# Query sums of squares fed into the projection stream, and rotary steps on 1024 columns

## The chip, the core and the metric

The kernel runs on one core of a Trainium2 chip. The metric is the device time of one execution in microseconds (us); the median of three runs is shown. PE is the matrix engine and PEld its weight loads, DVE the vector engine, ACT the scalar engine, POOL and SP the two other engines, which here issue transfers (DMAs) almost alone. Each engine works through its own queue in order, and a wait at the head of a queue holds up all that stands behind it.

## The reference, cut to what matters

One decoder layer on 1024 tokens of width 1024. The input is RMS-normalised and multiplied by one wide matrix (projections). Two mixers read the result:

```
# A: dilated attention, three groups (window, dilation) of 8 heads of 64
q_a, k_a = rope(q), rope(k)      # t * cos + rotate_half(t) * sin, per token position
o_a = sum over groups of softmax(q_a k_a^T / 8) v, weighted by the softmax denominators
# B: gated delta rule, 8 heads of 64, chunks of 64 tokens
gq = silu(conv(q)) / norm(gq) / 8 ; gk = silu(conv(k)) / norm(gk) ; gv = silu(conv(v))
t_inv = inverse(1 + a)           # a: unit lower triangular part of a chunk, 64 x 64
o_b = sequential scan over 16 chunks ; then RMS norm
merged = sigmoid(gate_a) * up_a(o_a * silu(z_a)) + sigmoid(gate_b) * up_b(o_b * silu(z_b))
out = rmsnorm(x + merged @ w_out)
```

The norm of gq needs a sum of squares over 64 channels for each head and token. In the rotary step, a head's 64 channels are two halves a and b: the results are a cos - b sin and b cos + a sin.

## The kernel before, in words

Matrices are split into two float16 parts, high and low, and each product is three matmuls. The projections are cut into *units* of 256 output columns. A unit is a generator; one *tick* of the `Feed` runs its next step: three matmuls on 512 columns in a unit of 28 steps (`Seven`, which forms seven products in place of eight) or in one of 32 (`Normal`). A unit's weights come by DMA on POOL's queue, and DVE and ACT split them (`whi`, `wlo`).

PE's order is written out by hand: what the code emits first runs first. Between steps of attention, of the delta rule's preparation and of its scan, the code calls `feed.tick(n)`, so the projections fill the time in which PE would wait for DVE and ACT. `feed.later(n, fn)` hangs a piece of work into the stream n ticks later, and `feed.flush()` ticks until nothing hangs there. The other engines' queues are ordered by a scheduler that goes by order in the code and by `high_priority`.

**Rotary step** (`rope_evict`, `rope_half`, L583 to L608). A unit of queries or keys gives four PSUM tiles of 512 columns: two halves of tokens, and in each the channel halves a and b. Each tile is copied out by ACT (`SC.copy`), or in a `Seven` unit with a remainder by DVE, into a buffer `rx` (three of 512 columns). For each half of the tokens DVE then does four products with the tables, two sums, and, for the results A and B each, ACT casts to float16 with the tokens reordered for the group's dilation (4 or 8: the source is read with a stride), and DVE subtracts the cast from the source, read with the same stride. There are 12 units and so 24 halves. `rope_out` sends the pieces by 16 and more DMAs on SP's queue.

**Attention** (`att_run`) runs the six sets of heads as a pipeline of scores, softmax (L776, L780), transposes (L790, L795) and values. In the last two sets `combine` merges the three groups on DVE, and `turn_out` (L876) transposes the result on PE `TURN_LAG` ticks after the set's values.

**Delta rule.** After attention and its flush, `decay`, `keys_side` and `solve` prepare the chunks; `solve` is a chain of small DVE steps at low priority, once per half of the heads, with a round trip through DRAM: `u_d` and `t_d` are stored and read back as `MT` (L1284) and `T1p` (L1282). `merge` (L1299, L1314) multiplies these on PE. The order of the code around the queries of half hb is:

```
state_side(0)                                  # loads, merge(0), products
for hb in 0, 1:
    feed.until(("gdn", hb, 0)); feed.tick(Q_LAG[hb])
    pairs(hb, qT, E[hb]); spill(hb)            # two times: 64 matmuls L1215, 4 ticks
    sumsq(hb, qT, rq...)                       # four times: 4 transposes L1196, square, sum, 2 ticks
    if hb == 0: feed.tick(STATE_LAG); state_side(1)
```

`sumsq` transposes into the PSUM tag "S" (two banks), ACT squares in place (L1201), DVE sums (L1202). The factors it gives are used in the scan, after its first tile of 128 tokens.

Of the kernel before, what the change touches and what calls it, by code (L numbers as in the profile page):

```python
# [10 lines left out]
F32 = mybir.dt.float32  # L11
# [3 lines left out]
ALU = mybir.AluOpType  # L15
# [42 lines left out]
ZS = 1  # L58
SCAN_LEAD = 6
OG = 2  # L60
TURN_LAG = 16
SUMS_AT = (4, 36, 68, 100)
MERGE_TICKS = 5
V_GAP = 8
# [12 lines left out]
def hybrid_block(ctx: ExitStack, tc: tile.TileContext, A):  # L77
# [498 lines left out]
    tabs = rp.tile([128, 2, S], F32, name="tabs")  # L576
    nc.sync.dma_start(out=tabs, in_=A["tabs"])
    amask = ap.tile([128, 384], F32, name="amask")
    nc.sync.dma_start(out=amask, in_=A["amask"])
    DIL = (1, 4, 8)  # L580

    def rope_evict(p, ct, offset=None, rest=None):
        with tc.high_priority(offset=offset):  # L583
            x = rp.tile([128, 512], F32, name="rx", tag="rx", bufs=3)
            if rest is None:
                SC.copy(x, p)  # L586
            else:
                STT(x, p, -1.0, rest, ALU.mult, ALU.subtract)
        return x

    def rope_half(g, pt, hf, ab, offset=0):
        d = DIL[g]
        ts = slice(hf * 512, hf * 512 + 512)
        with tc.high_priority(offset=offset):
            cos, sin = tabs[:, 0, ts], tabs[:, 1, ts]
            for n, (u, v, op) in (("A", (0, 1, ALU.subtract)), ("B", (1, 0, ALU.add))):
                t1 = rp.tile([128, 512], F32, name="rt1", tag="rt1", bufs=1)
                t2 = rp.tile([128, 512], F32, name="rt2", tag="rt2", bufs=1)
                TT(t1, ab[u], cos, ALU.mult)
                TT(t2, ab[v], sin, ALU.mult)  # L600
                o = rp.tile([128, 512], F32, name="ro", tag="ro", bufs=2)
                TT(o, t1, t2, op)
                ov = o.rearrange("p (n r) -> p r n", r=d)
                nn = 512 // d
                dst = [pt[n + x].rearrange("p (r n) -> p r n", r=d)[:, :, hf * nn:hf * nn + nn]
                       for x in "hl"]
                SC.copy(dst[0], ov)
                TT(dst[1], ov, dst[0], ALU.subtract)  # L608

    def rope_out(pt, pieces):  # L610

        with tc.high_priority():
            for name, dst, r0, _ in pieces:
                for hd in range(4):
                    nc.sync.dma_start(out=dst[r0:r0 + 32, hd], in_=pt[name][32 * hd:32 * hd + 32])
            for _, dst, r0, twice in pieces:
                if twice and r0:
                    nc.sync.dma_start(out=dst[64:128], in_=dst[0:64])

    def rope_tiles():  # L620
        return {n: rp.tile([128, S], F16, name=f"pc{n}", tag=f"pc{n}", bufs=1) for n in ("Ah", "Al", "Bh", "Bl")}

    def rope_unit(g, tiles, what):
        def start():
            pt = rope_tiles()
            pieces = pieces_of(tiles(), what)
            ab = {}

            def out(c, hf, p, rest=None):
                ab[c, hf] = rope_evict(p, c, rest=rest)  # L630
                if (1 - c, hf) in ab:
                    rope_half(g, pt, hf, [ab[0, hf], ab[1, hf]])
                if len(ab) == 4:
# [12 lines left out]

        return gen, gen7

    def rope_first(g, ws, pieces):

        pts = [rope_tiles(), {}]
        for n in "AB":
            both = ap.tile([128, 2, S], F16, name=f"pk{n}", tag="Vh" if n == "A" else "Vl", bufs=2)
            pts[1][n + "h"], pts[1][n + "l"] = both[:, 0], both[:, 1]
        for pt, banks in zip(pts, qk):
            rope_half(g, pt, 0, [rope_evict(p, ct, 0) for ct, p in enumerate(banks)], 0)
        ab = [q, [bank("S", 2), bank("S", 2)]]
        for i, u in ((2, 1), (3, 0), (3, 1)):
            for ct in range(2):
                quarter(ab[u][ct], ws[u], ct, i)  # L660
            if u == 0:

                with tc.high_priority():
                    for n in range(2):
                        feed.units[0][1].split(n)
        for pt, banks in zip(pts, ab):
            rope_half(g, pt, 1, [rope_evict(p, ct) for ct, p in enumerate(banks)])
        for pt, pc in zip(pts, pieces):
            rope_out(pt, pc)

# [16 lines left out]
    def v_unit(g, tiles):  # L687
        def start():
            vs = [ap.tile([128, 8, 256], F16, name=n, tag=n, bufs=2) for n in ("Vh", "Vl")]
            tiles().extend(vs)  # L690
            return vs

        def gen(w):
            wh, wl = w
            Vh, Vl = start()
            for jj in range(4):
                p = bank("mm", 3)
                for u in range(2):
# [12 lines left out]

        def gen7(w):
            vs = start()

            def out(c, hf, p, rest):
                cs = slice(128 * c, 128 * c + 128)
                vh, vl = [v[:, 4 * hf:4 * hf + 4, cs] if g == 0 else
                          v.rearrange("p (r h) c -> p r h c", h=2)[:, :, hf, cs] for v in vs]
                p = p.rearrange("p (i c) -> p i c", c=128)
                with tc.high_priority():  # L720
                    if rest is not None:
                        rest = rest.rearrange("p (i c) -> p i c", c=128)
                        x = rp.tile([128, 4, 128], F32, name="vx", tag="ro", bufs=2)
# [207 lines left out]
    def sums_of_h(k):  # L931

        x = {}
        for i in range(2):
            for j in range(2):
                x[i, j] = rp.tile([128, 512], F32, name="hx", tag=f"rt{j + 1}" if i == 0 else "ro", bufs=1 if i == 0 else 2)
# [252 lines left out]
    def sumsq(hb, src, dst, take=None):  # L1189

        for t0 in range(0, 8, 2):
# [11 lines left out]
            feed.tick(2)  # L1203

    def pairs(hb, src, dst):

# [396 lines left out]
    fp = ctx.enter_context(tc.tile_pool(name="fin", bufs=1))  # L1603
    late.append(fp)
# [243 lines left out]
def _constants():  # L1848
# [14 lines left out]
    ang = (np.arange(S, dtype=f)[:, None] * inv[None, :]).astype(f).astype(np.float64)  # L1863
    sc = H_SCALE * P_SCALE
    tabs = np.stack([np.tile(np.cos(ang).T, (4, 1)), np.tile(np.sin(ang).T, (4, 1))], axis=1) * sc
    q = p[:, None]
    k = p[None, :]
    prev = np.where(k >= q, 0.0, NEG)
# [81 lines left out]
```

## Time and profile before

| | |
|---|---|
| runs | 1096.77, 1093.91, 1096.39 us; median 1096.39 |
| profiled execution | 1097.13 us, of which the span of the trace is 1095.4 |
| PE busy | 1055.7 us, 96% |
| DVE busy | 871.8 us, 80% |
| ACT busy | 572.1 us, 52% |
| granted TensorE clock, mean | 0.995 |

The trace's times run from the start of the span. A row of a group of instructions gives count, busy time, mean duration in ns and the idle time just before them with what ended it. Matmuls overlap in PE, so a busy PE can hold short gaps, and the rows of waits give only those that left it idle.

### The profile page before, as it was taken

What the parts mean: (1) busy time and instruction counts of PE and PEld (TensorE: products, weight loads), DVE (VectorE), ACT (ScalarE), POOL (GpSimd) and SP (SyncE); (2) the same over time, 40 slices, a digit from 0 to 9 for tenths busy, and PEclk for the clock granted to TensorE, in tenths of its full rate; (3) what the DMA queues carried; (4) which work ended last, traced back from release to release, by engine and by line L of the source; (5) the groups of instructions that cost most, each with busy time, mean ns of one, the idle gap of its engine ahead of it and who ended that gap; (6) DMA issues with size and microseconds to landing.
All of it is one profiled execution on the core that took longest, in us unless ns stands there. A gap on an engine that the chain in (4) does not pass through costs nothing.

```text
span 1095.4 us, 23858 instructions
## 1 busy us (share of the span) xinstructions
PE 1055.7 (96%) x9426; PEld 641.1 (59%) x9426; DVE 871.8 (80%) x2039; ACT 572.1 (52%) x1296; POOL 65.4 (6%) x115
## 2 busy tenths in 40 slices
PE   6999999999999999989999999998999999999997
PEld 5895585775866855765555554544545554444443
DVE  5798997969879789979975797966478779699944
ACT  6455766667666656547745624234344335343522
POOL 1200000000000000000000000110200000000000
PEclk9999999999999999999999999999999999999999
DMA  8134521622626332641233357766585532763131
GB/s 290 62 94 138 137 64 66 165 81 81 146 67 164 82 115 75 153 111 56 74 121 138 97 137 186 238 214 174 156 280 159 159 113 88 256 224 127 69 131 77
DMA packets 99344, 146.89 MB, mean 134 GB/s; under 512 B 31120, under 2 KB 64400, under 8 KB 98336
## 3 DMA queue, kind: packets, MB, share of 16 engines
q1 hardware_dynamic: 68976, 83.10, 26.4%
q0 software_dynamic: 12320, 44.11, 13.1%
q10 hardware_dynamic: 17936, 18.16, 4.9%
q8 instruction: 74, 1.21, 0.5%
q14 instruction: 38, 0.31, 0.1%
HBM read 89.56 MB, written 36.90 MB: 115 GB/s over the span
## 4 chain that ended last, share of the span: by engine, by line
PE 57%; DVE 29%; ACT 7%; DMA 3%; issue 3%; SPq 1%; ACTq 0%; DVEq 0%
PE ps_mm L181 14%; PE ps_mm L183 13%; PE ps_mm L182 13%; DVE rt L85 3%; DVE wlo L82 3%; DVE ca L82 2%; DVE sm L776 2%; DVE tl L85 2%; DVE ro L85 2%; ACT sm L780 2%; DVE pcAl L85 1%; PE ps_S L183 1%; PE ps_S L182 1%; PE ps_S L181 1%; DVE pcBl L85 1%
## 5 line engine op out<-in xcount | busy, mean ns | idle before, releaser
L183 PE MATMUL ps_mm<-h_hi,wlo 128*128 128x512 f16 (+1 forms) x552 | 208.0, 377 | 0.0
L182 PE MATMUL ps_mm<-h_lo,whi 128*128 128x512 f16 (+1 forms) x492 | 185.3, 377 | 0.8 <-DVE h_lo L85 0.8
L181 PE MATMUL ps_mm<-h_hi,whi 128*128 128x512 f16 (+1 forms) x492 | 185.6, 377 | 0.0
L183 PEld LDWEIGHTS <-wlo 128*128 128x128 f16 x788 | 77.1, 98 | 87.7 <-issue 1.6
L182 PEld LDWEIGHTS <-whi 128*128 128x128 f16 x848 | 83.1, 98 | 71.6 <-issue 4.7
L181 PEld LDWEIGHTS <-whi 128*128 128x128 f16 x848 | 83.2, 98 | 70.6 <-issue 0.3
L181 PE MATMUL ps_mm<-whi,h_hi 128*128 128x256 f16 x384 | 105.7, 275 | 0.0
L182 PE MATMUL ps_mm<-wlo,h_hi 128*128 128x256 f16 x384 | 105.3, 274 | 0.0
L183 PE MATMUL ps_mm<-whi,h_lo 128*128 128x256 f16 x384 | 105.3, 274 | 0.0
L780 ACT ACTIVATE sm<-sm,osb 128x128 f32<-128x128 f32 (+1 forms) x160 | 69.7, 437 | 54.4 <-DVE osb L776 47.7
L85 DVE TENSOR_TENSOR tl<-ps_G,th 128x256 f16<-128x256 f32 (+1 forms) x96 | 51.9, 541 | 19.1 <-ACT th L795 19.0
L85 DVE TENSOR_TENSOR rt<-rx,tabs 128x512 f32<-128x512 f32 x96 | 64.5, 687 | 1.4 <-ACT rx L586 0.4
L776 DVE CUSTOM_DVE_ANT_0 sm<-ps_S,amask 128x128 f32<-128x128 f32 (+1 forms) x192 | 59.4, 347 | 7.0 <-PE ps_S L769 6.9
L82 DVE SCALAR_TENSOR_TENSOR wlo<-wstage,whi 128x1024 f16<-128x1024 f32 x50 | 60.9, 1219 | 3.7 <-ACT whi L164 3.6
L82 DVE SCALAR_TENSOR_TENSOR ca<-xc,cw,ca 128x512 f32<-128x512 f32 x72 | 53.8, 747 | 7.7 <-ACT ca L982 6.9
L790 PE MATMUL ps_G<-cons,sm 128*128 128x128 f32 x280 | 48.7, 276 | 4.5 <-ACT sm L780 3.0
L164 ACT ACTIVATE whi<-wstage 128x1024 f16<-128x1024 f32 x49 | 51.4, 1050 | 2.4 <-ACT gst L921 1.2
L790 PEld LDWEIGHTS ps_G<-cons,sm 128*128 128x128 f32 x280 | 35.6, 141 | 22.1 <-ACT sm L780 7.8
L82 DVE SCALAR_TENSOR_TENSOR whi<-wstage,whi 128x512 f16<-128x512 f32 x60 | 40.5, 687 | 9.3 <-ACT whi L328 8.4
L182 PEld LDWEIGHTS <-h_hi 128*128 128x128 f16 x384 | 45.9, 120 | 1.9
L181 PEld LDWEIGHTS <-h_hi 128*128 128x128 f16 x384 | 45.9, 120 | 1.8
L183 PEld LDWEIGHTS <-h_lo 128*128 128x128 f16 x384 | 45.8, 119 | 1.7
(438 smaller groups left out, 2601.0 us busy)
## 6 DMA issues: line engine op xcount, KB each, us to landing
wstage<-in_w POOLq DMA_DIRECT2D x68, 512.0 KB, 4.7
og<-osb ACTq DMA_DIRECT2D x32, 132.0 KB, 2.3
og<-og SPq DMA_DIRECT2D x32, 132.0 KB, 2.2
gspb<-gst ACTq DMA_DIRECT2D x16, 256.0 KB, 2.5
sga<-gspa SPq DMA_DIRECT2D x8, 512.0 KB, 6.6
wstage<-in_w_up POOLq DMA_DIRECT2D x8, 512.0 KB, 5.6
wos<-in_w_out SPq DMA_DIRECT2D x8, 512.0 KB, 4.1
sgb<-gspb SPq DMA_DIRECT2D x8, 512.0 KB, 5.3
```

Of the source, the lines that this page charges most:

```text
L82: (eng or V).scalar_tensor_tensor(out, in0, scalar, in1, op0=op0, op1=op1)
L85: (eng or V).tensor_tensor(out, in0, in1, op)
L164: in_turn(SC.activation(hi[:, 4 * c:4 * c + 4], st, AF.Copy, scale=W_SCALE))
L181: PE.matmul(out, lhsT=wh(k), rhs=mh(k), start=first and i == 0, stop=False, skip_group_check=True)
L182: PE.matmul(out, lhsT=wh(k), rhs=ml(k), start=False, stop=False, skip_group_check=True)
L183: last_pe[0] = PE.matmul(out, lhsT=wl(k), rhs=mh(k), start=False, stop=last and i == len(ks) - 1, skip_group_check=True).ins.name
L776: V.tensor_tensor_reduce(P[:, u, :128 * nk], psc[:, u * 256:u * 256 + 128 * nk], mask, -cexp, -NEG, ALU.add, ALU.min, accum_out=osb[:, 256 ...
L780: SC.activation(P[:, u, :128 * nk], P[:, u, :128 * nk], AF.Exp, bias=osb[:, 256 + hd:257 + hd], scale=-1.0, accum_out=osb[:, 260 + hd:261 ...
L790: PE.transpose(pt[:, c:c + 128], P[:, u, i * 128:i * 128 + 128], ident)
```

## The change

Three constants change, and one is new: `Q_LAG` from (10, 4) to (14, 4), `TURN_LAG` from 16 to 20, `Q_SUMS` is (8, 3). The sums of squares of the queries no longer stand in the code with ticks between them: `sumsq_steps` hangs their four steps 1, 9, 17 and 25 ticks later for the first half of the heads and 1, 4, 7 and 10 ticks later for the second, and each transposes into the one bank of the tag "O". A flush stands before the scan. The keys' sums stay as they were.

The rotary step reorders the tokens when it copies a PSUM tile out: the copy reads PSUM in order and writes with a stride. Its buffer holds a and b together (two buffers of 2 x 512 columns). The products take 1024 columns in one instruction, the second one in place; the two sums stay at 512 columns; cast and subtraction take A and B in one instruction of 1024 columns, in order. The tables' tokens are reordered too, so there is one table for each group, and it is loaded (1 MB) when the group's first unit starts. The first gate unit stages its results in one buffer of its own, where it used the two of the rotary sums.

```diff
-Q_LAG = (10, 4)
+Q_LAG = (14, 4)
+Q_SUMS = (8, 3)
-TURN_LAG = 16
+TURN_LAG = 20
+    def load_tabs(g):
+        if g not in tabs:
+            tabs[g] = rp.tile([128, 2, S], F32, name=f"tabs{g}", tag="tabs", bufs=1)
+            nc.sync.dma_start(out=tabs[g], in_=A["tabs"][g])
+    def rope_room():
+        return rp.tile([128, 2, 512], F32, name="rx", tag="rx", bufs=2)
-    def rope_evict(p, ct, offset=None, rest=None):
+    def rope_evict(g, x, p, ct, offset=None, rest=None):
+        by = lambda y: y.rearrange("p (n r) -> p n r", r=DIL[g])
+        x = x[:, ct].rearrange("p (r n) -> p n r", r=DIL[g])
         with tc.high_priority(offset=offset):
-            x = rp.tile([128, 512], F32, name="rx", tag="rx", bufs=3)
             if rest is None:
-                SC.copy(x, p)
+                SC.copy(x, by(p))
             else:
-                STT(x, p, -1.0, rest, ALU.mult, ALU.subtract)
+                STT(x, by(p), -1.0, by(rest), ALU.mult, ALU.subtract)
...
-            for n, (u, v, op) in (("A", (0, 1, ALU.subtract)), ("B", (1, 0, ALU.add))):
-                t1 = rp.tile([128, 512], F32, name="rt1", tag="rt1", bufs=1)
-                t2 = rp.tile([128, 512], F32, name="rt2", tag="rt2", bufs=1)
-                TT(t1, ab[u], cos, ALU.mult)
-                TT(t2, ab[v], sin, ALU.mult)
-                o = rp.tile([128, 512], F32, name="ro", tag="ro", bufs=2)
-                TT(o, t1, t2, op)
-                ov = o.rearrange("p (n r) -> p r n", r=d)
...
-                SC.copy(dst[0], ov)
-                TT(dst[1], ov, dst[0], ALU.subtract)
+            cos, sin = [tabs[g][:, i:i + 1, ts].to_broadcast([128, 2, 512]) for i in range(2)]
+            t = rp.tile([128, 2, 512], F32, name="rt", tag="rt", bufs=1)
+            TT(t, x, cos, ALU.mult)
+            TT(x, x, sin, ALU.mult)
+            TT(t[:, 0], t[:, 0], x[:, 1], ALU.subtract)
+            TT(t[:, 1], t[:, 1], x[:, 0], ALU.add)
...
+            SC.copy(dst[0], src)
+            TT(dst[1], src, dst[0], ALU.subtract)
...
-    gpool = [rp, "ro", 2]
+    gpool = [rp, "gst", 1]
...
+    def sumsq_steps(hb, src, dst):
+        def step(t0):
+            p = bank("O", 1)
...
+            with tc.high_priority():
+                SC.activation(p, p, AF.Square)
+                V.tensor_reduce(dst[:, t0:t0 + 2], ..., AX.X, ALU.add)
+        for n in range(4):
+            feed.later(Q_SUMS[hb] * n + 1, lambda n=n: step(2 * n))
...
-        sumsq(hb, qT, rq[:, :, 4 * hb:4 * hb + 4])
+        sumsq_steps(hb, qT, rq[:, :, 4 * hb:4 * hb + 4])
...
     feed.until(("gate", 5))
-    assert not feed.late
+    feed.flush()
```

## Rows read from the trace of the kernel before

**Rows 1.** The page: span, and busy time of the engines with its share.
```profile
span 1095.4 us, 23858 instructions
PE 1055.7 (96%) x9426; PEld 641.1 (59%) x9426; DVE 871.8 (80%) x2039; ACT 572.1 (52%) x1296; POOL 65.4 (6%) x115
```
**Rows 2.** Windows of 25 us: busy time of each engine, granted clock, DMA share.
```profile
425.00:450.00 25.00, 22.84 (x171) 13.48 (x169) 24.96 (x70) 15.98 (x40) 2.11 (x4) 1.00 0.51 135
725.00:750.00 25.00, 20.32 (x212) 10.32 (x211) 16.35 (x26) 10.52 (x19) 4.73 (x8) 0.98 0.96 271
975.00:1000.00 25.00, 25.00 (x117) 11.35 (x116) 25.00 (x49) 11.17 (x22) 0.00 (x0) 1.00 0.47 165
```
**Rows 3.** PE's waits: line and releaser, total us, times, longest.
```profile
PE ps_G L790 <- ACT sm L780: 3.0, 5, 0.8
PE ps_G L876 <- DVE f L82: 2.2, 1, 2.2
PE ps_O L817 <- DVE tl L85: 2.2, 4, 0.9
PE ps_S L1196 <- DVE rq L1202: 2.2, 1, 2.2
PE ps_S L181 <- ACT rx L586: 1.7, 1, 1.7
PE ps_G L876 <- DVE mx L85: 1.5, 1, 1.5
PE ps_G L876 <- DVE osb L85: 1.4, 1, 1.4
PE ps_S L1215 <- ACT qT L993: 1.3, 1, 1.3
PE ps_S L1196 <- DVE E L85: 1.2, 1, 1.2
PE ps_mm L181 <- ACT rx L586: 0.7, 1, 0.7
```
**Rows 4.** ACT's timeline: copies and casts at the start, and one cast of dilation 1.
```profile
39.12 0.58 ACT L586 COPY rx<-ps_S 128x512 f32<-128x512 f32 x1 [1.25 <-PE ps_S L476]
48.66 1.12 ACT L607 CAST pcAh<-ro 128x512 f16<-128x512 f32 x1
49.68 0.58 ACT L586 COPY rx<-ps_S 128x512 f32<-128x512 f32 x1
424.71 0.62 ACT L607 CAST pcAh<-ro 128x512 f16<-128x512 f32 x1
```
**Rows 5.** Windows around the two stretches at a lower clock; columns as in rows 2.
```profile
473.00:476.00 3.00, 3.00 (x25) 2.27 (x24) 2.73 (x9) 0.43 (x2) 0.00 (x0) 0.50 0.72 161
749.00:752.00 3.00, 3.00 (x11) 1.68 (x10) 1.35 (x3) 1.81 (x5) 0.00 (x0) 0.54 1.09 376
```
**Rows 6.** The second merge: SP's timeline, PE's, and what the tile T1p's view says of landing.
```profile
738.57 4.53 SPq L1282 DMA_DIRECT2D T1p<-t_d  x1
757.47 1.20 PE L1299 MATMUL ps_S<-T1p,MT 32*32 32x32 f32 x64
DMA to landing us min/median/max: 3.1/7.5/11.9
```
**Rows 7.** Groups of instructions by form: count, busy us, mean ns, idle before.
```profile
L85 DVE TENSOR_TENSOR rt<-rx,tabs 128x512 f32<-128x512 f32 x96 | 64.5, 687 | 1.4 <-ACT rx L586 0.4
L85 DVE TENSOR_TENSOR pcAl<-ro,pcAh 128x512 f16<-128x512 f32 x22 | 20.8, 944 | 0.6 <-ACT pcAh L607 0.5
L85 DVE TENSOR_TENSOR As<-As,bsc 128x1024 f32<-128x1024 f32 x4 | 4.9, 1217 | 0.0
L1202 DVE TENSOR_REDUCE rq<-ps_S 128x8 f32<-128x512 f32 x8 | 5.5, 689 | 6.9 <-ACT ps_S L1201 6.9
```
**Rows 8.** The first gate unit's staging buffer gst, timelines of DVE and SP.
```profile
395.95 0.68 DVE L82 SCALAR_TENSOR_TENSOR gst<-ps_mm,x 128x512 f32<-128x512 f32 x1
395.04 2.65 SPq L923 DMA_DIRECT2D gspa<-gst  x2
```

More of the change, by code (lines that the diff above doesn't have):

```diff
@@ L575, in hybrid_block @@
     rp = ropex.enter_context(tc.tile_pool(name="rope", bufs=1))
-    tabs = rp.tile([128, 2, S], F32, name="tabs")
-    nc.sync.dma_start(out=tabs, in_=A["tabs"])
+    tabs = {}
+    def load_tabs(g):
+        if g not in tabs:
+            tabs[g] = rp.tile([128, 2, S], F32, name=f"tabs{g}", tag="tabs", bufs=1)
+            nc.sync.dma_start(out=tabs[g], in_=A["tabs"][g])
+    load_tabs(2)
     amask = ap.tile([128, 384], F32, name="amask")
@@ L580, in hybrid_block, with rope_half @@
     DIL = (1, 4, 8)
[L582 removed]
+    def rope_room():
[3 more added lines that the diff above has]
+        x = x[:, ct].rearrange("p (r n) -> p n r", r=DIL[g])
         with tc.high_priority(offset=offset):
[L584 removed]
             if rest is None:
[L586 removed]
+                SC.copy(x, by(p))
             else:
[L588 to L591 removed]
+                STT(x, by(p), -1.0, by(rest), ALU.mult, ALU.subtract)
+    def rope_half(g, pt, hf, x, offset=0):
         d = DIL[g]
@@ L614, in rope_out @@
                 for hd in range(4):
-                    nc.sync.dma_start(out=dst[r0:r0 + 32, hd], in_=pt[name][32 * hd:32 * hd + 32])
+                    nc.sync.dma_start(out=dst[r0:r0 + 32, hd], in_=pt[name[1]][32 * hd:32 * hd + 32, "AB".index(name[0])])
             for _, dst, r0, twice in pieces:
@@ L620, in rope_tiles @@
     def rope_tiles():
-        return {n: rp.tile([128, S], F16, name=f"pc{n}", tag=f"pc{n}", bufs=1) for n in ("Ah", "Al", "Bh", "Bl")}
+        return {n: rp.tile([128, 2, S], F16, name=f"pc{n}", tag=f"pc{n}", bufs=1) for n in "hl"}
     def rope_unit(g, tiles, what):
         def start():
+            load_tabs(g)
             pt = rope_tiles()
             pieces = pieces_of(tiles(), what)
-            ab = {}
+            x, n = {}, [0]
             def out(c, hf, p, rest=None):
[L630 to L633, printed above, removed]
+                first = hf not in x
+                if first:
+                    x[hf] = rope_room()
+                rope_evict(g, x[hf], p, c, rest=rest)
+                if not first:
+                    rope_half(g, pt, hf, x[hf])
+                n[0] += 1
+                if n[0] == 4:
                     rope_out(pt, pieces)
@@ L649, in rope_first, with half @@
     def rope_first(g, ws, pieces):
[L651 to L654, printed above, removed]
+        pts = [rope_tiles(), {n: ap.tile([128, 2, S], F16, name=f"pk{n}", tag="V" + n, bufs=2) for n in "hl"}]
+        def half(pt, banks, hf, *offset):
+            x = rope_room()
+            for ct, p in enumerate(banks):
+                rope_evict(g, x, p, ct, *offset)
+            rope_half(g, pt, hf, x, *offset)
         for pt, banks in zip(pts, qk):
-            rope_half(g, pt, 0, [rope_evict(p, ct, 0) for ct, p in enumerate(banks)], 0)
+            half(pt, banks, 0, 0)
         ab = [q, [bank("S", 2), bank("S", 2)]]
@@ L666, in rope_first @@
         for pt, banks in zip(pts, ab):
-            rope_half(g, pt, 1, [rope_evict(p, ct) for ct, p in enumerate(banks)])
+            half(pt, banks, 1)
         for pt, pc in zip(pts, pieces):
@@ L722, in out @@
                         rest = rest.rearrange("p (i c) -> p i c", c=128)
-                        x = rp.tile([128, 4, 128], F32, name="vx", tag="ro", bufs=2)
+                        x = rope_room()[:, 0].rearrange("p (i c) -> p i c", c=128)
                         STT(x, p, -1.0, rest, ALU.mult, ALU.subtract)
@@ L934, in sums_of_h @@
         for i in range(2):
+            room = rp.tile([128, 2, 512], F32, name="hx", tag="rt" if i == 0 else "rx", bufs=1 + i)
             for j in range(2):
-                x[i, j] = rp.tile([128, 512], F32, name="hx", tag=f"rt{j + 1}" if i == 0 else "ro", bufs=1 if i == 0 else 2)
+                x[i, j] = room[:, j]
                 ts = slice(512 * j, 512 * j + 512)
@@ L1203, in sumsq @@
             feed.tick(2)
+    def sumsq_steps(hb, src, dst):
+        def step(t0):
+            p = bank("O", 1)
+            for t in (0, 1):
+                for c in range(2):
+                    o = (2 * t + c) * 128
+                    PE.transpose(p[:, o:o + 128],
+                                 src[2 * hb + c][:, 2 * (t0 + t):2 * (t0 + t) + 2].rearrange("p c i -> p (c i)"), ident)
+            with tc.high_priority():
+                SC.activation(p, p, AF.Square)
+                V.tensor_reduce(dst[:, t0:t0 + 2], p.rearrange("p (t h c) -> p t h c", t=2, c=64), AX.X, ALU.add)
+        for n in range(4):
+            feed.later(Q_SUMS[hb] * n + 1, lambda n=n: step(2 * n))
     def pairs(hb, src, dst):
@@ L1865, in _constants @@
     tabs = np.stack([np.tile(np.cos(ang).T, (4, 1)), np.tile(np.sin(ang).T, (4, 1))], axis=1) * sc
+    tabs = np.stack([tabs.reshape(128, 2, 2, 512 // d, d).swapaxes(3, 4).reshape(128, 2, S) for d in (1, 4, 8)])
     q = p[:, None]
```

7 lines of the change are left out of this document (3 added, 4 removed).

## The prediction, on record before the run

> **What bounds the kernel now.** I read the page's busy line first: PE is busy for 1055.7 us of a span of 1095.4, DVE for 80%, ACT for 52% [rows 1]. Then the windows of 25 us. Late in the run a window holds 117 matmuls of 512 columns with PE full: 25 / 117 = 0.214 us each, so a tick of three costs 0.64 us [rows 2]. The number of matmuls and transposes doesn't change, so what can be won is the time in which PE waits. The view of PE's waits lists it: ten waits there belong to the code that is changed or to the attention beside it [rows 3]. They sit where PE is not full: 425 to 450 us (DVE busy for 24.96 of 25 us) and 725 to 750 us [rows 2]. Last I looked at the clock: after the two longest of these waits the window's granted clock is 0.50 and 0.54, the lower of TensorE's two levels (1.2 against 2.4 GHz) [rows 5]. Each costs about half of 3 us and a little at the edges: some 1.7 us beside the wait itself.
>
> The sum below is made against the profiled execution's own 1097.13 us (span 1095.4 and 1.7 around it), which is 0.7 us over the median of the runs, 1096.39.
>
> **The change part by part.**
>
> *Rotary work, DVE.* Per half of tokens DVE had four products and two sums at 0.687 us and two subtractions at 0.944 us [rows 7]: 6.0 us, in 24 halves 144 us. Now it has two products and one subtraction of 1024 columns at 1.217 us, the price of a product of that size elsewhere [rows 7], and two sums at 0.687: 5.0 us, 121 us in all. Some 23 us of DVE go. ACT's two casts (1.12 us with a strided source, 0.62 without one [rows 4]) become one of 1024 columns. Against it, the copies out of PSUM now write with a stride; before, no operation does that. Below, a copy costs its 0.58 us, above, it doubles as the strided cast did against the plain one, to 1.1 us [rows 4]. I take the upper end, as the stride is that of the cast. This lies on ACT and DVE, which PE covers, apart from the start (next).
>
> The strided cast took 1.12 us against 0.62 for the plain one [rows 4]. The Trainium skill has a rule for it ("Advanced Engine Details and Errata", Memory Cachelines): an access that goes to another line of 16 bytes than the one before pays a penalty. It speaks of accesses and not of reads alone, so by it the change halves the strided passes and doesn't end them. The trace bears it out for reads; no run so far shows the write side. By the rule the start's term below is -1.2 us, by the plain copy's price -1.7.
>
> *Start.* PE waits 1.7 us for the second bank of keys [rows 3]: its copy, ready with the first at 39.12, starts at 49.68, behind a cast and for want of a third `rx` buffer to come free [rows 4]. Two buffers of pairs hold queries and keys at once, so the wait goes. In return up to three slower copies stand ahead of the split of the last tokens, whose lateness PE feels: 0 to 1.2 us. I take -1.2 (from -1.7 to -0.5).
>
> *Turn-outs.* PE waits 2.2 + 1.5 + 1.4 = 5.1 us at L876 for the merge on DVE [rows 3]. Four more ticks are at least 2.6 us, more where attention's own matmuls lie between, so each wait alone is covered, and so is the slow clock of 473 to 476 us: -6.8. What is late next: PE comes 1.5 us earlier to the later turn-out while DVE is full there [rows 2], so I keep 1.0 us as residual. The last set's flush runs four ticks more, useful work. Taken: -5.8 (-6.8 to -2).
>
> *Other copy wait.* 0.7 us at the copy of a rotary tile [rows 3] goes with the roomier buffers: -0.7 (-0.7 to 0).
>
> *One staging buffer in the first gate unit.* The second transfer out is issued at 395.04 and the next DVE result is wanted at 395.95 [rows 8]; with one buffer it waits for the landing, 1 to 2 us, and ACT after it as long. Behind them stand a softmax step and a cast for attention. PE has banks in hand: +0.7 (0 to 3).
>
> *Tables.* Two loads of 1 MB more on SP, a unit's 24 ticks (15 us) ahead of their use, after readers that finished a unit earlier: 0 (0 to 1).
>
> *Sums of squares, first half.* The lag of 14 covers the wait of 1.3 us for the last query tile. The waits of 1.2 us (a bank of "S" still read by the pairs) and 2.2 us (a bank before the sum is done) [rows 3] go, since the steps are 8 ticks (5.1 us) apart in another bank; with the clock at 749 to 752 us: -6.4.
>
> *What is late next there.* Behind the sums stood `state_side(1)` with the second merge. PE reaches it 4 ticks sooner (8 go, 4 are added: 2.6 us), 4.7 us of waits sooner, 1.7 us of slow clock sooner and with three steps of transposes (1.3 us) still to come: 757.47 - 10.3 = 747.2 us. Its operand T1p is loaded by a transfer issued at 738.57, the slowest of its four, 11.9 us to landing: 750.5 us [rows 6]. So a wait that the trace doesn't show had 7.0 us of cover and now has none: 3.3 us. The load ends a chain (decay, keys, two solves, a store, a load) that begins after attention's flush, now 4 ticks later against PE's stream, so up to 2.6 us more; an idle of this size has brought the lower clock twice, 1.7 us. Between 3.3 and 7.6 us I take 7.0, nearest to the upper end, since the chain's start is certain to move. Below, if the load lands 3 us sooner without the sums' traffic in its way, 0.3.
>
> *Sums, second half.* Steps are three ticks (1.9 us) apart on one bank; a sum takes 0.69 us after 0.86 us of idling for its square [rows 7], 1.6 in all. That is close, so +0.3 (0 to 1.5).
>
> *Attention beside the rotary steps.* PE's waits for softmax and its cast are 3.0 + 2.2 = 5.2 us [rows 3]. DVE is 23 us freer, but its pieces are longer (1.217 us in place of 0.687). -1.0 (-4 to +4).
>
> Sum: -1.2 - 5.8 - 0.7 + 0.7 - 6.4 + 7.0 + 0.3 - 1.0 = -7.1. 1097.13 - 7.1 = 1090.0 us.
>
> **The rivals.**
>
> *The merge's load is in time* (faster still). If DMA is less crowded from 740 to 755, since the sums no longer hold up the E products and the stores behind them, the 7.0 us become about 1: 1084 us. For it: the load's 11.9 us are far above its median of 7.5 [rows 6]. Against it: its place on SP's queue depends on solve, which doesn't get faster.
>
> *The waits come back* (no change). PE runs ahead of a DVE that is full from 425 to 450 us [rows 2], and half of the turn-outs' 6.8 us returns (+2.4 over my term); the merge's load lands another 3 us late behind the same stores: 1090.0 + 5.5 = 1095.5 us. That the sums, although hung into the stream, only pass their wait on is part of this case. For it speaks that both stretches are bound by chains outside PE; against it, that DVE gets 2 of its 23 us in that stretch.
>
> *Longer DVE pieces hold up attention* (slower). Each of 72 instructions of 1024 columns is 0.53 us longer than what stood there; softmax's subtraction (L776) and the cast's rest wait behind them, and PE behind those. If all were felt, 38 us. It decides from about 10.4 us on, which is 27% of them (my gain of 7.1 and the 3.3 us of 0.3%); at 40%, 15 us in place of the -1.0: 1097.1 - 6.1 + 15 = 1106 us. For it: DVE at 24.96 of 25 us [rows 2]. Against it: PE's waits for the softmax's cast are 2.2 us in the whole run [rows 3], although weight splits of the same length stand there already.
>
> **How the numbers follow.** Forecast, 0.52: 1090 us, its own range 1087 to 1094. Load in time, 0.16: 1084 (1081 to 1087). Waits come back, 0.22: 1095.5 (1093 to 1099). Longer pieces, 0.10: 1106. Below 0.1 goes at either end: the range is 1083 to 1098. A difference of 0.3%, 3.3 us, is about what a measurement of this kernel can tell from none. Faster by more (under 1093.1): the second case and nearly nine tenths of the first, 0.62. Within: the rest of the first and most of the third, 0.27. Slower (over 1099.7): 0.11.
>
> **What would show it.** Right: DVE's busy time near 850 us; no wait of PE at L876 and L1196 over 1 us; a wait of PE at L1299 of 3 to 6 us with the lower clock behind it; the copies of dilation 4 and 8 at 1.1 us; none at the start for the keys' bank. Wrong: PE's waits at L790 and L817 growing past 10 us in all (longer pieces), or PE full at the second merge (load in time). The prediction falls if waits at L876 stay as they were, or if the second merge's wait is longer than all that the sums gave back.

## The result and the profile after

The changed kernel takes 1084.93 us (median; 1084.07 to 1086.11), the kernel before 1096.24 beside it: ratio 0.9908 [0.9889, 0.9927]. The medians are 11.3 us apart; by the ratio it is 10.1 (8.0 to 12.2). The forecast was 1090.0 us and faster; the time lies inside the range of 1083 to 1098 and 2.1 us under the likeliest case's own, 1087 to 1094. The profiled execution took 1084.88 us, 12.25 less than the 1097.13 against which the sum was made; the sum said 7.1 less.

The page of the changed kernel, span and engines; it answers to [rows 1]:
```profile
span 1083.1 us, 23724 instructions
PE 1052.6 (97%) x9426; PEld 641.4 (59%) x9426; DVE 854.9 (79%) x1967; ACT 559.6 (52%) x1272; POOL 66.5 (6%) x115
```
DVE fell by 16.9 us, ACT by 12.5. Its windows, the first two at the times of [rows 2], the last two where the clock is low; columns as there:
```profile
425.00:450.00 25.00, 23.80 (x188) 15.27 (x186) 24.65 (x66) 14.12 (x36) 2.11 (x4) 1.00 0.57 147
725.00:750.00 25.00, 23.28 (x408) 12.67 (x407) 20.30 (x30) 12.19 (x24) 2.17 (x4) 1.00 0.76 215
42.60:46.00 3.40, 3.40 (x18) 2.40 (x18) 3.40 (x7) 1.04 (x1) 0.57 (x1) 0.51 0.10 18
104.10:107.50 3.40, 3.40 (x13) 1.48 (x12) 1.47 (x5) 1.41 (x8) 0.00 (x0) 0.50 0.00 0
```
The two stretches at the lower clock of [rows 5] are gone and two have come, at the start and at the first scores. The waits of PE in the changed kernel, which answer to [rows 3]:
```profile
PE ps_O L835 <- DVE tl L86: 2.7, 3, 1.3
PE ps_S L787 <- DMA Ql<-Ql: 2.3, 1, 2.3
PE ps_mm L184 <- issue: 1.2, 1, 1.2
PE ps_G L808 <- ACT sm L798: 1.0, 3, 0.4
PE ps_mm L183 <- DVE h_lo L86: 1.0, 1, 1.0
PE ps_mm L182 <- DVE rx L83: 1.0, 1, 1.0
PE ps_mm L182 <- ACT h_hi L434: 0.9, 1, 0.9
```
L835 and L808 are the former L817 and L790. The turn-outs, the sums (L1196), their bank (L1215) and the keys' bank are off the list; new are the first scores' wait for `Ql`, one of 0.9 us for the split's cast at the start and one of 1.0 us for DVE's copy of a rotary tile, at 441 us. The wait for the split's rest (`h_lo`), 1.0 us here, was 0.8 in the kernel before. The second merge answers to [rows 6]: SP's timeline at the last load of T1p and PE's at the first matmuls on it.
```profile
730.70 2.97 SPq L1317 DMA_DIRECT2D T1p<-t_d  x1
738.86 1.46 PE L1334 MATMUL ps_S<-T1p,MT 32*32 32x32 f32 x64
```
The tile's view, of the four T1p loads:
```profile
DMA to landing us min/median/max: 6.1/8.3/10.0
```
By the transfer's events T1p landed at 739.08 us. The batch of 64 matmuls begins 0.2 us before that, and no wait for T1p is listed.

Where the time came from is read by comparing the starts of the same projection matmul in two traces: the stream is the same in all kernels, so the change of the difference over a stretch is what that stretch won. The stretches are in the time of the kernel before; us won, losses negative; "forecast" is the prediction's terms that fall there:

| stretch | forecast | whole change | TURN_LAG alone | rotary alone | sums alone |
|---|---|---|---|---|---|
| 0 to 53, start | +1.2 | -0.3 | +0.4 | +0.4 | +0.2 |
| 53 to 107, first scores | 0 | -3.2 | 0.0 | -0.7 | 0.0 |
| 107 to 400, attention (and gst) | +0.3 | +5.9 | -0.1 | +5.3 | 0.0 |
| 400 to 600, turn-outs | +6.5 | +5.0 | +4.7 | +2.0 | +1.9 |
| 600 to end, sums and merge | -0.9 | +5.2 | +4.0 | +0.7 | -0.5 |
| sum | +7.1 | +12.6 | +9.1 | +7.6 | +1.6 |

Each column is one execution against one execution (12.6 us by the matmuls, 12.25 by the executions). The sums' +1.9 lies where that part changes nothing, so single entries of 1 to 2 us say little; timed ratios decide.

### The profile page after: what moved, and what is told of

Its sections match the earlier page's. It is cut to its first block, busy times and chain, and to the rows that moved or that the text cites. A ratio compares the mean times of both kernels' runs of the same rounds, so it can differ in the third digit from the quotient of the medians.

```text
span 1083.1 us, 23724 instructions
## 1 busy us (share of the span) xinstructions
PE 1052.6 (97%) x9426; PEld 641.4 (59%) x9426; DVE 854.9 (79%) x1967; ACT 559.6 (52%) x1272; POOL 66.5 (6%) x115
## 4 chain that ended last, share of the span: by engine, by line
PE 59%; DVE 26%; DMA 5%; ACT 4%; issue 3%; SPq 2%; ACTq 0%; DVEq 0%
PE ps_mm L182 14%; PE ps_mm L184 14%; PE ps_mm L183 14%; DVE ca L83 4%; DVE wlo L83 2%; DVE X L86 2%; DVE stmp L86 2%; DVE sm L794 2%; DVE rt L86 2%; PE ps_S L182 1%; PE ps_S L184 1%; PE ps_S L183 1%; DVE tl L86 1%; PE ps_G L808 1%; SPq L624 1%
## 5 line engine op out<-in xcount | busy, mean ns | idle before, releaser
L86 DVE TENSOR_TENSOR tl<-ps_G,th 128x256 f16<-128x256 f32 (+1 forms) x96 | 51.8, 540 | 21.5 <-ACT th L813 21.0
L808 PE MATMUL ps_G<-cons,sm 128*128 128x128 f32 x280 | 47.5, 275 | 2.1 <-ACT sm L798 1.0
L329 ACT ACTIVATE whi<-wstage 128x512 f16<-128x512 f32 x60 | 37.1, 626 | 18.5 <-DVE wstage L328 13.4
L182 PE MATMUL ps_mm<-h_hi,wlo 128*128 128x512 f16 x120 | 45.6, 380 | 1.0 <-DVE rx L83 1.0
```

What stands on the lines that cost most here:

```text
L86: (eng or V).tensor_tensor(out, in0, in1, op)
L182: PE.matmul(out, lhsT=wh(k), rhs=mh(k), start=first and i == 0, stop=False, skip_group_check=True)
L329: in_turn(SC.activation(t[:, b, 0], self.part[name], AF.Copy, scale=W_SCALE))
L808: PE.transpose(pt[:, c:c + 128], P[:, u, i * 128:i * 128 + 128], ident)
```

## The experiments

Twelve kernels ran, four at a time, each set beside the kernel before on the same chip (1096.32, 1095.94 and 1095.26 us).

**turn.** The lag of the turn-outs alone.
```diff
-TURN_LAG = 16
+TURN_LAG = 20
```


> The kernel before with TURN_LAG = 20 alone. Theory (the lag took the turn-outs' waits away): PE's three waits at L876 (5.1 us) and the lower clock at 473 us (1.7 us) go, 0 to 1.5 us come back at the later turn-out: 1089 to 1091.5 us, 5 to 7 us under before. Rival (DVE was full, and only the lighter rotary steps took the waits away): PE stays at L876 for most of the 5.1 us, 1094 to 1096 us. In both the first scores don't wait for Ql and the waits at L1196 stay (3.4 us and the lower clock after them).

1089.15 us, ratio 0.9939 [0.9923, 0.9955], in the 1089 to 1091.5 expected. No wait at the turn-outs and no lower clock before the last 10 us. More than half of the change's gain is this constant. The waits for the sums at L1196 stay, 2.2 and 0.6 us, but in this execution no lower clock follows them. The next fence shows that it also reorders SP's queue (issue time, time in the queue, transfer): first the kernel before, then this one.
```profile
723.97 0.33 SPq L1275 DMA_DIRECT2D u_d<-X  x1
728.77 0.50 SPq L1276 DMA_DIRECT2D t_d<-T  x1
```
```profile
719.47 0.33 SPq L1275 DMA_DIRECT2D u_d<-X  x1
721.58 0.33 SPq L1276 DMA_DIRECT2D t_d<-T  x1
```
Before, two loads `rvt` and a load `kbt` that waits for u_d's landing stand between the two stores; now the `rvt` loads go ahead of both stores, and `t_d` leaves 3.9 us after the solve's end in place of 6.6.

**sums.** The sums part alone.
```diff
-Q_LAG = (10, 4)
+Q_LAG = (14, 4)
+Q_SUMS = (8, 3)
-        sumsq(hb, qT, rq[:, :, 4 * hb:4 * hb + 4])
+        sumsq_steps(hb, qT, rq[:, :, 4 * hb:4 * hb + 4])
```


> The kernel before with the sums of squares of the queries hung into the stream alone (Q_LAG 14, Q_SUMS, flush). On SP's queue the load of rvt and a load of kbt still stand between the second solve's two stores, as before. Theory (that order set T1p's landing): the waits at L1215 and L1196 and the lower clock at 749 us go (6.4 us), PE comes to the second merge near 747 us and waits there for T1p until about 750.5, 2 to 5 us with the lower clock after it: 1091 to 1095 us. Rival (the load was late because of the sums' and pairs' own traffic): T1p lands before 748, no wait over 1 us at the merge, 1089 to 1091 us.

1097.01 us, ratio 1.0008 [0.9992, 1.0025]: nothing won, above the 1091 to 1095 expected. PE's timeline at the second merge:
```profile
744.22 0.24 PE L1316 MATMUL ps_S<-T1p,MT 32*32 32x32 f32 x2
748.90 1.91 PE L1316 MATMUL ps_S<-T1p,MT 32*32 32x32 f32 x62 [4.44 <-DMA T1p<-t_d]
```
A window behind it, columns as in [rows 2]:
```profile
747.70:754.50 6.80, 5.60 (x71) 3.19 (x72) 3.64 (x5) 1.01 (x3) 0.00 (x0) 0.50 0.73 249
```
This is the wait that the prediction's +7.0 described: PE comes 13 us sooner than in [rows 6], waits 4.4 us for T1p, and runs 6.8 us at half clock, 3.4 lost.

**rope.** The rotary part alone (all of the diff from `load_tabs` to `gpool`).

> The rotary part alone (rotary steps, tables, staging buffer), TURN_LAG 16 and the sums as before. Theory: it gains what PE waited for softmax and its cast between 100 and 300 us (5 to 6 us), loses 3.2 us at the first scores (Ql copied late, lower clock) and 0 to 1.5 us at the start, and leaves the waits at L876 and L1196: 1093 to 1096 us. Rival (the lighter DVE is what took the turn-outs' waits away): waits at L876 under 1.5 us in all, 1087 to 1090 us.

1093.12 us (1089.6 to 1096.0), ratio 0.9976 [0.9961, 0.9991], in the 1093 to 1096 expected: 2.6 us, less than the 7.6 of the one execution in the table. Attention wins 5.3 us there, and PE then comes earlier to a turn-out whose merge on DVE isn't done. The waits of PE between 104 and 450 us:
```profile
PE ps_G L893 <- DVE osb L85: 3.7, 1, 3.7
PE ps_O L834 <- DVE tl L85: 0.5, 1, 0.5
PE ps_G L807 <- ACT sm L797: 0.5, 2, 0.2
```
That wait was 1.4 us before [rows 3]; it is 3.7 now, with the lower clock for 3.4 us behind it, and 3.6 us are lost from 400 to 452 us. In the 48 us after that 5.6 are won, since the wait of 2.2 us [rows 3] and the lower clock [rows 5] are gone. So the turn-outs' stretch wins 2.0 us in this execution, and nothing shows that they take back what the rotary steps win in attention. By the times the rotary part is worth as much beside the longer lag as alone: 0.9914 for *rope_turn* against 0.9939 for *turn* is a ratio of 0.9975.

**turn_sums.** Both, without the rotary part (the two diffs above).

> TURN_LAG 20 and the sums hung into the stream, rotary steps as before. With the longer lag the loads of rvt stand ahead of the second solve's stores on SP's queue, in place of between them. Theory (order on SP): T1p lands 3 us or more sooner against PE than in the run with the sums alone, the second merge waits under 1 us, and the two gains add up: 1083 to 1087 us. Rival (traffic, not order): the merge waits 2 us or more as with the sums alone, 1087 to 1090 us.

1089.59 us, ratio 0.9942 [0.9920, 0.9963], the same as the lag alone and above the 1083 to 1087 expected. PE reaches the merge at 740.38 us, T1p landed at 736.84: the wait of the kernel *sums* is gone, as the theory had it, but the gains don't add up; the time is the rival's.

**rope_turn.** The changed kernel without the sums part (`Q_LAG` 10, `sumsq` in one piece).

> The changed kernel with the sums of squares as before (Q_LAG 10, ticks between the steps). Theory (with the load of T1p early, the sums' waits of 3 to 5 us with their clock are what the hung steps win): 1087 to 1089 us, 2 to 4 over the changed kernel, with waits at the sums' transposes of 2 to 3.5 us. Rival (what the sums win they lose again at the second merge, as in the pair of runs without the rotary part): within 1 us of the changed kernel.

1085.50 us, ratio 0.9914 [0.9893, 0.9936] beside 0.9908: the sums part is worth nothing that these runs can tell from zero, though PE's waits at L1214 for the sums (2.2 and 1.2 us) are back in its profile. That is the rival's time, under the 1087 to 1089 expected. The ratios of the rotary part and the lag multiply: 0.9976 x 0.9939 = 0.9915.

**stride_late.** The changed kernel, wide steps kept, but the tokens reordered in cast and subtraction again; the copies out of PSUM are plain.
```diff
-        by = lambda y: y.rearrange("p (n r) -> p n r", r=DIL[g])
-        x = x[:, ct].rearrange("p (r n) -> p n r", r=DIL[g])
+        by = lambda y: y
+        x = x[:, ct]
...
-            src = t.rearrange("p a (r n) -> p a r n", r=d)
+            src = t.rearrange("p a (n r) -> p a r n", r=d)
```


> The changed kernel with the tokens reordered where they were before: copies out of PSUM and tables in plain order, cast and subtraction of 1024 columns read with a stride. Theory (the stride costs about as much on either side): copies 0.58 us, the strided cast and subtraction near 2.1 us each in 16 of 24 halves, so DVE some 12 us busier than in the changed kernel; no wait for the split at the start and no lower clock there (3 to 3.5 us won), the waits for Ql at the first scores grow to 3 us or more, and attention loses 1 to 3 of its 6 us: 1083 to 1087 us. Rival (the number of instructions is what counts, not the stride): attention keeps all, 1081 to 1083 us.

1099.66 us, ratio 1.0045 [1.0027, 1.0064]: slower than before, and a miss by more than 12 us. Its page:
```profile
PE 1054.5 (96%) x9426; PEld 640.0 (58%) x9426; DVE 865.8 (79%) x1967; ACT 566.6 (52%) x1272; POOL 66.5 (6%) x115
```
The cast's group by form:
```profile
L616 ACT CAST pch<-rt 128x1024 f16<-128x1024 f32 x22 | 37.4, 1698 | 33.8 <-DVE rt L86 30.0 <-DMA Ql<-pcl 3.7
```
Two of PE's waits between 100 and 300 us:
```profile
PE ps_G L808 <- ACT sm L798: 7.0, 11, 2.1
PE ps_O L831 <- ACT osb L840: 2.6, 3, 1.4
```
ACT's timeline at one of the second kind:
```profile
217.81 2.02 ACT L616 CAST pch<-rt 128x1024 f16<-128x1024 f32 x1 [2.44 <-DMA Ql<-pcl]
219.73 0.36 ACT L840 COPY osb<-ps_O 128x256 f32<-128x256 f32 x1
```
DVE and ACT do 6 us *less* than in the kernel before [rows 1], and PE still loses 15.7 us against the changed kernel between 107 and 300 us. A cast of 1024 columns read with a stride is one piece of 2.0 to 2.2 us (1.05 in order), and all three waits for `osb` stand behind one. DVE's subtraction, read with the same stride, is a piece of 2.0 to 2.1 us (1.22 in order), and the softmax's step on DVE stands behind it:
```profile
229.40 2.02 DVE L86 TENSOR_TENSOR pcl<-rt,pch 128x1024 f16<-128x1024 f32 x1 [1.81 <-ACT pch L616]
231.33 0.28 DVE L794 CUSTOM_DVE_ANT_0 sm<-ps_S,amask 128x128 f32<-128x128 f32 x1
```
Of the eleven waits for `sm`, four (3.6 us) follow such a cast, five (2.6 us) such a subtraction and two neither. This is the prediction's rival of the longer pieces, at 2 us a piece and on both engines. The changed kernel has the same buffers and pieces no longer than those of a weight split, 1.05 us on ACT and 1.22 on DVE, and escapes it.

**narrow.** The changed kernel with 512-column products, casts and subtractions; the order still made at the eviction.
```diff
-            TT(t, x, cos, ALU.mult)
-            TT(x, x, sin, ALU.mult)
+            for a in range(2):
+                TT(t[:, a], x[:, a], cos[:, 0], ALU.mult)
+                TT(x[:, a], x[:, a], sin[:, 0], ALU.mult)
...
-            SC.copy(dst[0], src)
-            TT(dst[1], src, dst[0], ALU.subtract)
+            for a in range(2):
+                SC.copy(dst[0][:, a], src[:, a])
+                TT(dst[1][:, a], src[:, a], dst[0][:, a], ALU.subtract)
```


> The changed kernel with the rotary steps in 512 columns again but the tokens still ordered at the eviction: two products of 0.69 in place of one of 1.22 (24 pairs of these), two casts of about 0.62 in place of one of 1.05 and two subtractions of 0.69 in place of one of 1.22 (22 each): DVE +7 us, ACT +4 us, no piece longer than 1.1 us. Theory: what the attention stretches gained (about 5 us between 107 and 300 us) comes mostly from the order at the eviction, which takes the strided reads out of cast and subtraction, so most stays: 1086 to 1088 beside 1084.9. Rival one: the width is what pays: 1089 to 1091. Rival two: shorter pieces block ACT and DVE less, so it is as fast or faster: 1083 to 1085.

1084.65 us, ratio 0.9904 [0.9885, 0.9923], against 0.9908: the width pays nothing that can be measured. That is the time of rival two, under the 1086 to 1088 of the theory. Two of its groups by form:
```profile
L86 DVE TENSOR_TENSOR pcl<-rt,pch 128x512 f16<-128x512 f32 x44 | 29.4, 686 | 6.9 <-DMA Qh<-Qh 4.0 <-DMA Ql<-pcl 1.2 <-ACT pch L618 1.1
L618 ACT CAST pch<-rt 128x512 f16<-128x512 f32 x44 | 27.0, 620 | 24.4 <-DVE rt L86 21.5 <-DVE osb L796 2.9
```
Its DVE is busy for 860.7 us, 5.8 more than in the changed kernel. By the stretches attention keeps 3.6 of the 5.9 us (2.3 lost), a later wait at 470 us with the lower clock costs 2.9, and the wait for `Ql` doesn't come, 4.2 won. So the order at the eviction carries most of attention's gain; the width's part shows in one trace and not in the times.

**v1.** The changed kernel with two changes of order: ACT's copies of the first keys' banks behind the split of the last tokens, and on SP the first keys' DMAs behind the queries' pieces.
```diff
+                e = SC.copy(x, by(p))
+                if after:
+                    tc.add_manual_dep(e.ins, after, order_only, reason="behind the split")
...
+        queries = rope_out(pts[0], pieces[0])
+        rope_out(pts[1], pieces[1], after=queries)
```


> The changed kernel with two orders set: the two copies of the first keys behind the split of the last tokens on ACT, and the first keys' transfers behind all of the first queries' on SP. Theory (the slow copies and the late copy of Ql cost 3.5 and 3.2 us with their lower clocks): no lower clock before 400 us, the split's cast at 39 us in place of 40.1, Ql's copy issued before 90 us and no wait at the first scores: 1078 to 1081 us. Rival (what is won at the start is lost again, since attention then waits for the keys or softmax): 1083 to 1085 us.

1082.42 us, ratio 0.9881 [0.9859, 0.9904], just above the 1078 to 1081 expected. ACT's timeline at the start, the changed kernel and then v1:
```profile
36.09 1.97 ACT L599 COPY rx<-ps_mm 128x512 f32<-128x512 f32 x2
38.41 1.94 ACT L599 COPY rx<-ps_S 128x512 f32<-128x512 f32 x2 [0.35 <-PE ps_S L477]
40.14 1.05 ACT L434 CAST h_hi<-xs 128x1024 f16<-128x1024 f32 x1
```
```profile
36.08 1.96 ACT L601 COPY rx<-ps_mm 128x512 f32<-128x512 f32 x2
38.97 1.04 ACT L436 CAST h_hi<-xs 128x1024 f16<-128x1024 f32 x1 [0.93 <-DVE xs L83]
40.13 1.93 ACT L601 COPY rx<-ps_S 128x512 f32<-128x512 f32 x2
```
The split starts 1.2 us sooner, the 3.4 us at the lower clock go, and the start wins 2.8 us. The second change did nothing: `Ql` is issued at 89.96 in place of 95.30 us, but lands at 100.18, 10.2 us later instead of 7.3, and PE, 2.5 us earlier itself, waits the same 2.3. So the interleaving of queries and keys on SP, which I held for the cause, isn't enough. At the second merge v1 loses 1.4 us against the changed kernel: it comes 3.0 us sooner, MT lands no sooner, and a new wait is listed.
```profile
PE ps_G L1358 <- DMA MT<-u_d: 2.0, 1, 2.0
```

**v2.** v1 with both T1p loads ahead of the MT loads on SP, and the MT loads in the order 1, 3, 0, 2.
```diff
-        for kb in range(4):
-            b = kb % 2
-            if b == 0:
-                nc.sync.dma_start(out=T1p[...], in_=t_d[kb]...)
+        for kb in (0, 2):
+            nc.sync.dma_start(out=T1p[...], in_=t_d[kb]...)
+        for kb in (1, 3, 0, 2):
+            b = kb % 2
```


> As v1, and T1p is loaded ahead of MT for each merge. Theory (PE meets T1p's landing at the second merge with no cover, so some executions wait): T1p lands 2 to 4 us before PE comes; 0 to 2 us under v1, and a smaller spread of the runs. Rival (T1p is in time anyway): the same as v1 within 1 us.

1079.66 us, ratio 0.9861 [0.9837, 0.9885]: 2.8 us under v1, more than the 0 to 2 expected, though the two intervals overlap; the runs spread as widely (3.8 us against 4.0). Against v1 the trace wins 2.7 us, 2.6 of them at the second merge: the last MT lands 3.6 us earlier (739.42 against 743.02) and T1p 1.2, and the wait for MT is gone. So v1's merge was bound by SP's queue. In the changed kernel no wait for MT is listed, and against it v2 wins 1.2 us there.

**v3.** v2 with the two copies of the queries' second half-rows (512 KB each) ahead of the last eight DMAs of the first keys; the other engines' orders are the same.

> The second version with one thing moved: on SP's queue the two copies of the queries' second half-rows (Qh<-Qh, Ql<-Ql, 512 KB each) go ahead of the last eight DMAs of the first keys; the other four engines' orders stay as they are. In the second version they are issued at 88.5 and 89.9 us, together with a weight load (88.96 us), and the first scores wait 2.3 us for Ql<-Ql, after which the clock is at half for 3.4 us (1.7 us lost). Theory: the copies share the DMA engines with the weight load, and issued before it (83 to 86 us) they land before 95 us: wait and lower clock go, 2.3 + 1.7 = 4.0 us, 1079.7 to 1075.7 (1074.5 to 1077). Rival: the DMA engines are full either way and the last keys' pieces, now behind the copies, are what the first scores wait for: 1079 to 1081, with a wait for a Ks DMA at the first scores.

1078.38 us, ratio 0.9850 [0.9837, 0.9864]: above the 1074.5 to 1077 expected, and no longer apart from v2 in time. SP's timeline, v2 and then v3:
```profile
88.50 1.32 SPq L635 DMA_DIRECT2D Qh<-Qh  x1
89.86 0.60 SPq L635 DMA_DIRECT2D Ql<-Ql  x1
```
```profile
82.68 0.59 SPq L635 DMA_DIRECT2D Qh<-Qh  x1
83.31 0.59 SPq L635 DMA_DIRECT2D Ql<-Ql  x1
```
In v3 `Ql` lands at 89.48 us, 6.2 after its issue, with the weight load of 88.92 still to come; in v2 it lands at 100.42, 10.6 after it, beside weight loads issued at 88.96 and 93.10. Wait and lower clock are gone from v3's trace, no wait for the keys has come, and that stretch wins 3.1 us. What the DMA engines did in v2 from 90 to 92 us, queue by queue (packets, MB, share of the engines; q0 is POOL's queue with the weights, q1 SP's with the copies):
```profile
q0 software_dynamic: 85, 0.35, 73.5%
q1 hardware_dynamic: 5, 0.01, 1.1%
```
So the copies, issued at 88.50 and 89.86 us, share the DMA engines with the weights and stand while these go. In time, 1.2 us are left of it, inside the two intervals.

**v3_whole.** v3 without the sums part.
```diff
-Q_LAG = (14, 4)
+Q_LAG = (10, 4)
-        sumsq_steps(hb, qT, rq[:, :, 4 * hb:4 * hb + 4])
+        sumsq(hb, qT, rq[:, :, 4 * hb:4 * hb + 4])
```


> The third version without the sums part of the change (the queries' sums of squares in one piece again, Q_LAG 10). In the changed kernel this part was worth nothing (1085.5 without it, 1084.9 with it). Theory: its gain (the 2.2 and 1.2 us that PE waits for the sums) is given back at the second merge, which comes that much earlier and finds T1p or MT not landed; in the third version T1p is loaded some 3 us earlier and nothing is given back, so that undoing the part costs 3 to 4 us: 1078.5 to 1080 beside 1075.7. Rival: the sums' waits cost nothing in the timed runs, since something else sets the pace there: within 1 us of the third version.

1083.19 us, ratio 0.9889 [0.9876, 0.9903], 4.8 us slower than v3 and above the 1078.5 to 1080 expected. Its longest wait of PE at the sums:
```profile
PE ps_S L1224 <- DVE rq L1230: 2.2, 1, 2.2
```
The window behind it:
```profile
734.40:737.80 3.40, 3.40 (x12) 1.78 (x10) 1.45 (x3) 1.89 (x4) 0.00 (x0) 0.50 1.07 368
```
The sums part, worth nothing that could be told in the changed kernel, is worth 4.8 us in v3. By the traces it wins 4.9 us here from 600 to 925 us and 2.4 there. Of the 2.5 between them 1.7 are the lower clock behind this wait, which didn't follow the same wait of 2.2 us in *rope_turn*'s execution, and 0.8 are the merge, which v3 passes that much faster than the changed kernel. So the theory of the loads covers the smaller part in the traces, and why the times differ by more is open.

**ropesums.** The changed kernel with the lag of 16.

> The changed kernel with TURN_LAG 16 in place of 20 alone. SP's order in the second solve's round trip is then that of the kernel before (t_d stored behind rvt, rvt and kbt), and T1p lands about 28 us after the solve's end in place of 23. Theory: the turn-outs' waits come back (3.7 and 1.5 us with the clock lost behind them, 5.5 to 6), and the second merge, reached as early as in the changed kernel, waits 4 to 5 us for T1p with a lower clock behind it: 1092 to 1096, no faster than the rotary part alone (1093.1). Rival: SP's order has nothing to do with the merge, the lag is worth the turn-outs alone: 1090 to 1091.5, and no wait for T1p in the profile.

1093.61 us, ratio 0.9980 [0.9960, 1.0001], as expected no faster than the rotary part alone. Three of PE's waits:
```profile
PE ps_G L894 <- DVE osb L86: 3.7, 1, 3.7
PE ps_G L1349 <- DVE Y L86: 1.7, 2, 1.2
PE ps_S L1334 <- DMA T1p<-t_d: 0.3, 1, 0.3
```
The window behind the merge:
```profile
751.80:758.60 6.80, 5.63 (x130) 2.93 (x117) 4.08 (x6) 2.49 (x6) 0.00 (x0) 0.50 0.13 52
```
The old order on SP is back, and 4.1 us are lost in the merge's stretch, but not as I wrote: T1p costs 0.3 us here. The last MT lands at 750.49 us, after PE's second batch begins at 749.41, and the waits of 1.7 us for `Y` and 6.8 us of lower clock go with the rest.

## Why the prediction was right in sign and 5 us too slow

The second merge in nine kernels, us after the second solve's end (T1p by its events, PE by its first matmul there):

| kernel | SP's order | t_d stored | T1p landed | PE arrives |
|---|---|---|---|---|
| before | old | 6.6 | 28.3 | 35.3 |
| sums | old | 6.6 | 28.8 | 24.1 |
| rope | old | 5.7 | 25.4 | 34.4 |
| ropesums | old | 5.6 | 25.4 | 24.9 |
| turn | new | 3.9 | 19.1 | 30.6 |
| turn_sums | new | 4.0 | 19.9 | 23.5 |
| rope_turn | new | 3.9 | 21.5 | 31.1 |
| after | new | 3.9 | 23.4 | 23.2 |
| v2 | new, T1p first | 3.9 | 20.8 | 23.4 |

- **The step that failed: "a wait ... had 7.0 us of cover and now has none", taken at +7.0.** PE's arrival was worked out rightly: 747.2 us; measured 738.9, which is 746.3 in the time of the kernel before (its stream was 7.4 us ahead by then). But T1p's landing was carried over from the old trace, "its place on SP's queue depends on solve, which doesn't get faster". It landed 23.4 us after the solve in place of 28.3, or at 746.5 against the 750.5 to 753 of the prediction. So PE stays ahead of the landing by 0.2 us, close to the 0.3 that the prediction gave for an early load, and no wait for T1p is listed. The place depends on the queue's order too: 25.4 to 28.8 us in the four kernels with the old order, 19.1 to 23.4 in those with the new one, which the lag of the turn-outs brings. Of the 4.9 us between the kernel before and the changed one the order makes 2.0 (*ropesums* against the changed kernel) and the rotary part alone, in the old order, 2.9 (*rope*), for which no run gives the reason; these are single executions, and the order alone makes 9.2 in *turn*. Where the order is old, PE early and the rotary part as before (*sums*), the forecast wait is there in full; in *ropesums* it is 0.3. Why the queue's order turns at 20 ticks is not settled.
- **Sums: -6.4 taken.** The waits are off the list as forecast, but what the part is worth isn't: 0.6 us by the times in the changed kernel (*rope_turn*), which is inside the intervals, and 4.8 in v3. Of the 5.2 us that the changed kernel won from 600 us on, the lag alone won 4.0 in *turn*.
- **The rival's time, and half of its mechanism.** 1084 us was "load in time". Its reason, less crowded DMA, has something: the last T1p landed 8.4 us after issue, before 11.9 [rows 6]. The order of the stores is the other half.
- **Waits that come back** (1095.5): not in the changed kernel. With the lag of 16 beside the new rotary steps, in *rope* and *ropesums*, a turn-out waits 3.7 us, and the times are 1093.1 and 1093.6 us; the longer lag keeps that off.
- **Attention: -1.0 taken, -5.9 measured** (with the staging buffer's +0.7 in the same stretch; ACT waits 0.3 us for it). The term let the 23 us off DVE be offset by longer pieces. (The rotary groups gave 22.6 us back, but DVE's own strided copies cost 2.9 more, and DVE fell by 16.9 in all.) The pieces of 1.2 us cost nothing that *narrow* shows in the times, and *narrow* puts the gain on the order at the eviction.
- **Turn-outs -5.8 and other copy -0.7:** measured -5.0. The copy's wait of 0.7 us went, but one of 1.0 for DVE's copy of a rotary tile came. The tables and the sums' second half show no wait.
- **Start: -1.2 taken, +0.3 measured.** The keys' bank wait went (1.8 us won at 46 to 53 us), but "up to three slower copies stand ahead of the split" cost a wait of 0.9 us, 0.2 more at the split's rest and the lower clock, 2.8 in all, above the 1.2 allowed. *v1* shows it by undoing it. The copies took the upper end of their bounds, 1.97 us for two in a row against 0.58 for one [rows 4], although their stride is not "that of the cast": the cast read every 4th or 8th element, the copy writes 64 or 128 elements apart. The Trainium skill's rule on lines of 16 bytes ("Advanced Engine Details and Errata", Memory Cachelines) speaks of accesses; the trace agrees for writes too, 1.01 to 1.13 us a copy against 0.58.
- **Not foreseen at all:** the first scores, +3.2. *v3* names the cause.
- **How firm the first three stretches are.** Up to 400 us *rope*, *ropesums*, *rope_turn* and the changed kernel run the same instructions in the same order on every engine, so they are four executions of one thing. In this order attention won 5.3, 5.5, 5.5 and 5.9 us, the first scores lost 0.7, 3.3, 1.5 and 3.2, and the start brought +0.4, +0.4, -0.8 and -0.3. The waits at the start are the same in all four, those for `Ql` are 1.5 to 2.4 us; the rest is whether the lower clock follows: at the start in the last two, at the first scores in the second and the fourth.

By the table, 6.1 us (sums and merge) and 5.6 (attention) too little and 4.7 (start, first scores) and 1.5 (turn-outs) too much leave 5.5 us. That the forecast came this close is in part luck: errors of 11.7 and 6.2 us stand against each other.

## What to carry to other kernels

A constant that moves work on one engine can reorder another engine's queue: compare the order of the DMA queue, not only PE's, before a landing time is carried over from the old trace. Cost a rotary or softmax helper by its longest piece on the engine that feeds PE as well as by its sum: 6 us less work in pieces of 2 us was slower here, and pieces of 1 us were free. When a part gains nothing, try it again after other waits are gone: the sums went from 0.6 us, inside the intervals, to 4.8. And compare executions of the same order before a loss of 2 us is put down to a change.

## What the runs showed of the hardware

- A copy of 128x512 float32 out of PSUM on ACT that writes with a stride of 64 or 128 elements takes 1.01 to 1.13 us, in order 0.58. A cast of 128x1024 on ACT that reads with a stride of 4 or 8 elements takes 2.0 to 2.2 us, in order 1.05, and a subtraction on DVE with such a source 2.0 to 2.1, in order 1.22.
- PE's idling of 4.4 us in *sums* was followed by 6.8 us at a granted clock of 0.50; one of 2.3 us at the first scores by 3.4 us at 0.50 in the changed kernel, v1 and v2, and one of 2.4 us at the same place in *rope_turn* by none. The two waits at the start, 0.9 and 1.0 us, were followed by 3.4 us at about half clock in the changed kernel and *rope_turn* and by none in *rope* and *ropesums*. So a wait of 2.3 us can cost 4.0, and needn't.
- The same 512 KB copy within SBUF lands 6.2 us after its issue beside its twin (v3), and 10.2 to 10.6 beside two weight loads of 512 KB as well (v1, v2).

The version that is fastest, v3, beats both kernels: 0.985 of the kernel before, where the change alone makes 0.991.
